# RMSNorm and matrix product on one core: the first eight tiles of the output stored as one transfer

## The chip, the cores and the metric

The kernel runs on one core of a Trainium2 chip. The metric is the device time of one launch in microseconds (us). The core has five engines with a queue of instructions each: TensorE (PE) multiplies matrices and turns tiles round, VectorE (DVE), ScalarE (ACT) and GpSimd (POOL) work on elements, and SyncE (SP) only issues transfers. Transfers between memory and the core's SBUF are carried out by 16 DMA engines that all queues share. SP and ACT each have a ring of their own on every one of the 16. A transfer is cut into packets, here one contiguous run of a partition each, and its 128 partitions are spread evenly, 8 packets to an engine.

## The reference

```python
batch, seq, dim, out_dim = 16, 1024, 512, 768
rms = np.sqrt(np.mean(x ** 2, axis=-1, keepdims=True) + eps)
x_norm = x / rms * gamma
return np.matmul(x_norm, weight).astype(np.float32)
```

There are 16384 tokens of 512 features. Each token is divided by its root mean square, scaled by gamma and multiplied by a 512 x 768 matrix. All inputs and the output are 32-bit floats: 33.6 MB of x and 1.6 MB of weight come in, 50.3 MB go out.

## The kernel before

The tokens are cut into 128 tiles of 128. Which token lands in which tile is free as long as the load and the store agree, and the helper rows() (lines 140 to 142) settles it for both: a block of t tiles is read as "(p t) d", so that a partition holds t consecutive tokens and tile number k of the block is the k-th token of every partition. The larger t, the longer the contiguous run of a partition.

Gamma goes into the weight, which is cast to bf16 once. A tile then passes through these steps:

- load (line 177): tiles 0 to 7 in transfers of 2, 2 and 4 tiles, all later ones in transfers of 8. Tiles 0 to 31 are issued at the start on SP's queue. The twelve later loads are issued on ACT's queue, each about 28 tiles ahead of use, when the buffer xt that it fills (two halves of 16 tiles) is done with.
- cast to bf16 on GpSimd (line 188), eight or four tiles at a time. The last four tiles of each sixteen are cast by line 260 into xq instead.
- sums of squares on ScalarE (line 196), then root (line 201) and reciprocal (line 203).
- the turn of the tile: by TensorE through PSUM (line 230) and a copy by VectorE (line 239), or, for the four tiles in xq, by VectorE alone in 16 moves of 32 x 32 blocks (line 271), three moves to a pair of tiles.
- eight matmuls on TensorE (line 300) into one of three PSUM accumulators.
- the scale by the reciprocal root from PSUM into the output buffer ot, on ScalarE for even tiles and on VectorE for odd ones (lines 279 and 281).
- store (line 293) by SP.

The output buffer ot has three parts of eight tiles, so tile i writes where tile i - 24 stood and waits for the store of that tile. The main loop goes over pairs of tiles (j is the pair). The kernel's class Order writes down every operation with what it reads and writes, and puts waits on semaphores where one engine, or a transfer, needs another's result; each engine works in the order in which the operations were added. No planner changes that order.

Two tables say how transfers are grouped: x_first and x_size for loads, o_first and o_size for stores. A store is issued with the last tile of its stretch:

```python
if i == first + n - 1:
    src = ot[s][:, first % OG:first % OG + n, :]
    order.transfer(SP, lambda: SP.dma_start(out=rows(out, first, n), in_=src), reads=cells("ot", s, first % OG, n))
```

The stores before are of 1, 1, 2 and 4 tiles, then thirteen of 8, and at the end three of 4 and two of 2. In the loads of tiles 0 to 7 and the stores of the same tiles, each transfer's tokens are a block of their own (t is 2, 2 and 4). Tiles 8 to 15 have eight consecutive tokens to a partition, tiles 16 to 31 sixteen, all later ones 32.

Of the kernel before, what the change touches and what calls it, by code (L numbers as in the profile page):

```python
# [100 lines left out]
def kernel(  # L101
# [22 lines left out]
    XG, OG = 16, 8  # L124
    FIRST, START, LEAD = 2 * XG, 4, 14

    def stretches(group, parts):
        first, size, i = {}, {}, 0
        for g in range(NT // group):
            for n in parts.get(g, [group]):  # L130
                for t in range(i, i + n):
                    first[t], size[t] = i, n
                i += n
        return first, size

    last = NT // OG - 1
    x_first, x_size = stretches(OG, {0: [2, 2, 4]})
    o_first, o_size = stretches(OG, {0: [1, 1, 2, 4], last - 1: [4, 4], last: [4, 2, 2]})

    def rows(ap, i, n):  # L140
        base, t = (i - i % OG, OG) if OG <= i < XG else (x_first[i], x_size[i]) if i < OG else (i - i % XG, XG) if i < 2 * XG else (i - i % (2 * XG), 2 * XG)
        return ap[base * P:(base + t) * P, :].rearrange("(p t) d -> p t d", t=t)[:, i - base:i - base + n, :]

    def sb(name, shape, dtype):
# [29 lines left out]
    def load(i):  # L174
        dst, to = x_of(i, x_size[i])
        queue = SP if i < FIRST else ACT
        order.transfer(queue, lambda: queue.dma_start(out=dst, in_=rows(x, i, x_size[i])), writes=to)  # L177
# [110 lines left out]
    def store(i):  # L288
        first, n = o_first[i], o_size[i]
        s = first // OG % 3  # L290
# [3 lines that stand above are left out]
# [188 lines left out]
```

## Time and profile before

| | |
|---|---|
| median of 3 runs | 208.84 us (208.83 to 209.33) |
| the profiled execution | 209.07 us, span 207.1 us |
| granted TensorE clock | 0.993 |
| busy: PE, DVE, ACT, POOL | 194.7, 149.5, 144.3, 60.0 us |
| moved by DMA | 85.62 MB, 413 GB/s over the span |
| stores | 22 transfers, 5.8 to 25.6 us from issue to landing, median 22.1 |
| loads of x | 18 transfers, 3.4 to 23.8 us, median 18.1 |
| last store issued, landed | 200.4, 206.2 us |

Times in rows are microseconds from the span's start. A row of a window gives busy time and number of instructions of each engine, then the granted clock, the mean busy share of the 16 DMA engines and the GB/s that they moved; the share can come out slightly over 1, because a packet counts to the stretch in which it starts and neighbouring packets overlap a little. A row of the timeline gives start, duration, engine, line, operation, output and input, and in square brackets how long the engine was idle before it and what ended that. The trace also has a record of every DMA packet: its queue, size, start and duration.

### The profile page before, as it was taken

To read this page: it belongs to the slowest core of one execution; us is meant where nothing else is said; L and a number is where in the kernel's file an instruction comes from. 1 tells how busy PE (TensorE), PEld (TensorE's weight loads), DVE (VectorE), ACT (ScalarE), POOL (GpSimd) and SP (SyncE) were. 2 spreads that over 40 slices of the span, in tenths; PEclk is the share of its full clock that TensorE was granted. 3 is DMA by queue.
4 is the path that set the end of the run, shared out by engine and by line. 5 is a ranking of instruction groups with operands and counts; after the bars stand their busy time and mean duration, and the time that the engine had idled before them with its cause. 6 is when DMAs were issued, how large, how long until landed. Compare 5 with 4: busy or idle time off the path is not lost.

```text
span 207.1 us, 2794 instructions
## 1 busy us (share of the span) xinstructions
PE 194.7 (94%) x1236; PEld 72.7 (35%) x717; DVE 149.5 (72%) x255; ACT 144.3 (70%) x343; POOL 60.0 (29%) x34
## 2 busy tenths in 40 slices
PE   7789999999999999999999999999999989999940
PEld 1233434343334334433344333443343324333310
DVE  0446556999579975999579975999569964999530
ACT  4598898777777687777777687676949758683310
POOL 2156752157006340065105170060604224000000
PEclk9999999999999999999999999999999999999997
DMA  6999999999999999999999999999999999999992
GB/s 222 402 434 453 370 419 420 426 461 407 437 429 423 449 419 440 419 434 429 432 449 411 430 434 423 445 423 437 413 424 445 427 440 435 423 437 394 394 412 120
DMA packets 6064, 85.62 MB, mean 413 GB/s; under 512 B 674, under 2 KB 676, under 8 KB 1828
## 3 DMA queue, kind: packets, MB, share of 16 engines
q1 hardware_dynamic: 4320, 60.30, 68.9%
q10 hardware_dynamic: 1732, 25.17, 28.5%
q8 instruction: 7, 0.11, 0.2%
q14 instruction: 5, 0.04, 0.0%
HBM read 35.13 MB, written 50.33 MB: 413 GB/s over the span
## 4 chain that ended last, share of the span: by engine, by line
PE 71%; DMA 17%; DVE 5%; SPq 1%; issue 1%; POOL 1%; ACT 0%; ACTq 0%
PE ps L300 63%; DMA out_dram<-ot 12%; PE ps L230 8%; DMA xt<-in_x_dram 5%; DVE ot L281 2%; DVE xTq L271 2%; DVE xT L239 1%; POOL xb L188 1%; SPq L345 0%; ACT ot L279 0%; SPq L177 0%; DVE rstd L203 0%; SPq L477 0%; ACTq L93 0%; SPq L436 0%
## 5 line engine op out<-in xcount | busy, mean ns | idle before, releaser
L300 PE MATMUL ps<-w_bf,xT 128*128 128x512 bf16 (+1 forms) x800 | 147.9, 326 | 2.1 <-DVE w_bf L281 1.1
L279 ACT ACTIVATE ot<-ps,rstd 128x768 f32<-128x768 f32 x64 | 57.6, 899 | 48.5 <-PE ps L300 37.3
L196 ACT ACTIVATE jk<-xt 128x512 bf16<-128x512 f32 x128 | 78.7, 619 | 1.9 <-DMA xt<-in_x_dram 1.9
L188 POOL CAST xb<-xt 128x2048 bf16<-128x2048 f32 (+3 forms) x21 | 46.4, 2218 | 112.4 <-PE ps L230 69.0
L281 DVE TENSOR_SCALAR ot<-ps,rstd 128x768 f32<-128x768 f32 x64 | 64.8, 1013 | 9.5 <-PE ps L300 8.1
L296 PEld LDWEIGHTS <-xT 128*128 128x128 bf16 x400 | 39.3, 98 | 60.7 <-issue 52.8
L230 PE MATMUL ps<-ident_f,xb 128*128 128x128 f32 x200 | 54.4, 276 | 0.9 <-POOL xb L188 0.9
L239 DVE COPY xT<-ps 128x1024 bf16<-128x1024 bf16 (+1 forms) x53 | 34.5, 654 | 24.2 <-PE ps L230 22.5
L271 DVE STREAM_TRANSPOSE xTq<-xq 32x256 f32<-32x256 f32 x112 | 48.8, 435 | 3.4
L230 PEld LDWEIGHTS ps<-ident_f,xb 128*128 128x128 f32 x200 | 28.3, 143 | 46.6 <-issue 43.3
L300 PE MATMUL ps<-w_bf,xTq 128*128 128x512 bf16 x224 | 42.8, 326 | 0.0
L196 ACT ACTIVATION_READ_ACCUMULATOR jk<-xt 128x1 f32 x128 | 24.4, 190 | 0.0
L296 PEld LDWEIGHTS <-xTq 128*128 128x128 bf16 x112 | 11.0, 98 | 14.5 <-issue 14.5
L260 POOL CAST xq<-xt 128x2048 bf16<-128x2048 f32 x7 | 13.3, 1893 | 0.0
L203 DVE RECIPROCAL rstd<-rms 128x8 f32<-128x8 f32 (+3 forms) x20 | 3.9, 193 | 8.1 <-ACT rms L201 7.9
L201 ACT ACTIVATE rms<-ssq,eps_sb 128x8 f32<-128x8 f32 (+3 forms) x20 | 6.0, 300 | 0.6
L300 PE MATMUL ps<-warm 128*128 128x512 bf16 x10 | 4.5, 588 | 1.4 <-DVE eps_sb L354 1.4
L279 ACT ACTIVATE w_bf<-w_f,g_sb 128x768 bf16<-128x768 f32 x2 | 1.9, 935 | 1.8 <-DMA w_f<-in_weight_dram 1.8
L377 DVE COPY g_sb<-ps 128x4 f32<-128x4 f32 x1 | 0.2, 163 | 3.2 <-PE ps L371 3.2
L341 ACT ACT_TABLE_LOAD x1 | 1.3, 1283 | 1.5 <-SPq L436 1.5
L281 DVE TENSOR_SCALAR w_bf<-w_f,g_sb 128x512 bf16<-128x512 f32 (+2 forms) x3 | 1.4, 482 | 1.2 <-DMA w_f<-in_weight_dram 1.2
L371 PEld LDWEIGHTS ps<-ident_f,g_row 2*128 2x128 f32 x2 | 0.3, 200 | 2.6 <-issue 2.6
(10 smaller groups left out, 2.0 us busy)
## 6 DMA issues: line engine op xcount, KB each, us to landing
out_dram<-ot SPq DMA_DIRECT2D x13, 3072.0 KB, 22.7
xt<-in_x_dram ACTq DMA_DIRECT2D x12, 2048.0 KB, 18.8
xt<-in_x_dram SPq DMA_DIRECT2D x3, 2048.0 KB, 18.2
out_dram<-ot SPq DMA_DIRECT2D x4, 1536.0 KB, 10.9
out_dram<-ot SPq DMA_DIRECT2D x3, 768.0 KB, 6.8
w_f<-in_weight_dram SPq DMA_DIRECT2D x2, 768.0 KB, 5.9
xt<-in_x_dram SPq DMA_DIRECT2D x2, 512.0 KB, 5.4
xt<-in_x_dram SPq DMA_DIRECT2D x1, 1024.0 KB, 9.5
```

What stands on the lines that cost most here:

```text
L188: run(POOL, lambda: POOL.tensor_copy(out=xb[s][:, i % 8:i % 8 + n, :], in_=src), of, cells("xb", s, i % 8, n))
L196: run(ACT, lambda: ACT.activation(out=jk[j], in_=src[:, 0, :], func=AF.Square, accum_out=ssq[:, i:i + 1]), of, [("jk", j), ("ssq", i)])
L201: run(ACT, lambda: ACT.activation(out=rms[:, s], in_=ssq[:, s], func=AF.Sqrt, scale=1.0 / D, bias=eps_sb), [("ssq", t) for t in range(i, i ...
L203: run(DVE, lambda: DVE.reciprocal(out=rstd[:, s], in_=rms[:, s]), [("rms", i)], [("rstd", t) for t in range(i, i + n)])
L230: run(PE, lambda: PE.transpose(out=tp[b][:, t, h, :], in_=words[:, lo:lo + P], identity=ident_f), cells("xb", s, j % 4 * 2 + t) + ["ident" ...
L239: run(DVE, lambda: DVE.tensor_copy(out=dst[:, t:t + n, :], in_=src[:, t:t + n, :]), [("tp", b)], cells("xT", j % 4, t, n))
L260: run(POOL, lambda: POOL.tensor_copy(out=xq[s], in_=src), of, [("xq", s)])
L271: run(DVE, lambda: DVE.transpose(out=dst, in_=src), [("xq", s)], [("xTq", s)])
L279: run(ACT, lambda: ACT.mul(out=dst, in_=src, mul=r), reads, writes)
L281: run(DVE, lambda: DVE.tensor_single_scalar(out=dst, in_=src, scalar=r, op=mybir.AluOpType.mult), reads, writes)
L296: run(PE, lambda: PE.ldweights(lhsT), [cell])
L300: run(PE, lambda: PE.add_instruction(mybir.InstMatmult(name=nc.get_next_instruction_name(), engine=mybir.EngineType.PE, ins=[PE.lower_ap(r ...
```

## The change

The first group of stores, tiles 0 to 7, is no longer cut in four: it is one transfer of 3 MB, issued after tile 7. For that the eight tiles must be one block, so rows() gives them eight consecutive tokens to a partition, as tiles 8 to 15 have. The loads use the same helper. They stay three transfers of 2, 2 and 4 tiles with the same packet sizes (4, 4 and 8 KB), but each now fetches its part of a row of eight tokens, pieces that stand 16 KB apart in memory, where each used to fetch one solid stretch.

```diff
-    o_first, o_size = stretches(OG, {0: [1, 1, 2, 4], last - 1: [4, 4], last: [4, 2, 2]})
+    o_first, o_size = stretches(OG, {last - 1: [4, 4], last: [4, 2, 2]})
 
     def rows(ap, i, n):
-        base, t = (i - i % OG, OG) if OG <= i < XG else (x_first[i], x_size[i]) if i < OG else (i - i % XG, XG) if i < 2 * XG else (i - i % (2 * XG), 2 * XG)
+        t = OG if i < XG else XG if i < 2 * XG else 2 * XG
+        base = i - i % t
         return ap[base * P:(base + t) * P, :].rearrange("(p t) d -> p t d", t=t)[:, i - base:i - base + n, :]
```

The packets of a store are 3 KB times its tiles: those of the four early stores were 3, 3, 6 and 12 KB, that of the one transfer is 24 KB, as in every other store of eight tiles. The order of the instructions on PE, DVE, ACT and POOL stays; on SP four issues become one.

## The prediction

> **What bounds the kernel now.** I read the busy slices first, then the windows by stage, the waits of ScalarE, the queues, and last the trace's records of single DMA packets.
>
> ```profile
> PEclk9999999999999999999999999999999999999997
> DMA  6999999999999999999999999999999999999992
> DMA packets 6064, 85.62 MB, mean 413 GB/s; under 512 B 674, under 2 KB 676, under 8 KB 1828
> q1 hardware_dynamic: 4320, 60.30, 68.9%
> q10 hardware_dynamic: 1732, 25.17, 28.5%
> ```
>
> The 16 DMA engines are busy from the first slices to the last but one, and the two queues (q1 is SP's, q10 is ScalarE's) fill 97.4% of the span between them. The clock is full, so it is no suspect.
>
> ```profile
> core 0: us, PE busy (x) PEld busy (x) DVE busy (x) ACT busy (x) POOL busy (x), PEclk, DMA share, GB/s
> 20.00:30.00 10.00, 10.00 (x69) 4.19 (x41) 5.75 (x10) 9.31 (x26) 6.33 (x3) 1.00 1.00 398
> 150.00:160.00 10.00, 9.98 (x67) 3.96 (x39) 7.98 (x14) 6.49 (x17) 2.03 (x1) 1.00 1.01 433
> 160.00:170.00 10.00, 9.23 (x60) 3.10 (x32) 8.62 (x16) 6.18 (x16) 1.97 (x2) 1.00 1.01 432
> 190.00:200.00 10.00, 9.05 (x56) 2.64 (x27) 6.08 (x9) 3.59 (x4) 0.00 (x0) 1.00 0.94 393
> ```
>
> TensorE and the DMA engines are both full. TensorE loses 0.8 us in the middle (9.98 and 9.23 of 10), and ScalarE's rows (start, duration, idle time before and who ended it) say why:
>
> ```profile
> 143.19 0.90 ACT L279 ACTIVATE ot<-ps,rstd 128x768 f32<-128x768 f32 x1 [1.85 <-DMA out_dram<-ot]
> 155.59 0.90 ACT L279 ACTIVATE ot<-ps,rstd 128x768 f32<-128x768 f32 x1 [2.98 <-DMA out_dram<-ot]
> 168.01 0.90 ACT L279 ACTIVATE ot<-ps,rstd 128x768 f32<-128x768 f32 x1 [3.07 <-DMA out_dram<-ot]
> ```
>
> A group of eight tiles waits for the store that frees its output buffer, every 12.4 us: DMA can't keep pace with TensorE's 11.7 us per group.
>
> Which one ends last is told by the packet records. The last store is issued at 200.40 and lands 5.8 us later, at 206.2. Fifteen engines finish their last packet between 203.3 and 203.5; one runs without a gap from 201.98 to 205.74, sixteen 6 KB packets end to end. That engine is slower on the stores: its 24 KB packets take 0.944 us (median), those of the others 0.912. So the end is the work of one slow DMA engine, which is behind by 2.3 us and has nothing to wait for.
>
> **The change, part by part.** The sum is made against the profiled execution: span 207.1, time 209.07, which is 0.23 above the median of 208.84.
>
> *Stores removed and added.* Every transfer puts 8 packets on each engine. Packet medians are 121 ns (3 KB), 234 (6 KB), 460 (12 KB) and 912 (24 KB). Before: 16 x 0.121 + 8 x 0.234 + 8 x 0.460 = 7.49 us of an engine. After: 8 x 0.912 = 7.30. That is 0.19 less, and three semaphore records of 9 ns fewer are 0.03: 0.22 us on an ordinary engine. On the slow one the 12 KB packets of the early store take 0.474 on average and the small ones are not slower: 1.94 + 1.88 + 3.79 = 7.61 against 8 x 0.944 = 7.55, with the records 0.08 to 0.09 us. The end is the slow engine's, so the gain is between 0.08 and 0.22; I take 0.14, since the slow engine's handful of early packets is a thin sample.
>
> *SP's issues.* Four issues (12.48, 13.53, 17.05, 24.41; 0.33 us each) become one, after tile 7, at the same 24.41. SP has nothing else to do then; the next issue is at 36.23. Nothing.
>
> *When the bytes move.* The early stores do not move early now. They stand on SP's ring behind the loads of tiles 0 to 31, whose packets end at 26.84; the first 3 KB packet starts at 26.63. So issuing at 24.41 instead of 12.48 leaves no hole, provided that the new store is ready by 26.6: at the end of the run an idle engine took up the store issued at 200.40 at about 201.5, 1.1 us after, which gives 25.5. Cover: 1.1 us; if the loads end 0.5 us sooner, 0.6.
>
> *Who shares with whom.* The two rings take turns packet by packet: from 43.8 on the slow engine's records alternate 0.912-like and 0.611 (the 16 KB of a load), and eight rounds are 12.13 us, the distance of successive stores. Between 27 and 42 the stores' packets are small, so the loads run ahead: the first three on q10 run 27.46 to 33.11, 34.54 to 41.59 and, after 4 us with no load, 45.58 to 56.99. With 24 KB packets on the other ring each takes some 11.4 us and starts 12.13 after the one before: 27.5 to 38.9, to 51.0, to 63.1. Loads from the third on come 6.1 us later. The stores gain what they lose: that of tiles 8 to 15 ended at 55.65 and now ends near 26.7 + 2 x 12.13 = 51.0, 4.7 us sooner. No byte is added.
>
> *The stall that goes.* Stores 4.7 us sooner take away waits of 1.6 to 3.1 us on ot, and with them TensorE's 0.8 us. What is late next is the loads.
>
> *The wait that comes.* GpSimd takes a load as soon as it lands, and DVE takes what GpSimd cast:
>
> ```profile
> 169.60 1.89 POOL L188 CAST xb<-xt 128x2048 bf16<-128x2048 f32 x1 [8.03 <-DMA xt<-in_x_dram]
> 171.44 1.89 POOL L260 CAST xq<-xt 128x2048 bf16<-128x2048 f32 x1
> 177.74 1.36 DVE L271 STREAM_TRANSPOSE xTq<-xq 32x256 f32<-32x256 f32 x3
> ```
>
> The last load, tiles 120 to 127, is issued at 147.36 and lands at 169.5; 6.1 later is 175.6. Two casts take it to 179.4, where DVE wanted the last quad at 177.7, or 176.9 with the 0.8 us gone: DVE waits 1.7 to 2.5 us. Behind that wait in its queue stand the copy xT<-ps (TensorE's transposes wait for it) and the odd tiles' scale. DVE is full from there to 193, so I count all of it: last store issued between 200.4 - 0.8 + 0 and 200.4 - 0.8 + 2.5, that is 199.6 to 202.1. An undisturbed last store needs 1.1 us to start, 8 x 0.234 = 1.9 to move and up to 0.5 to land, so 203.1 to 205.6, under the slow engine's 206.2 - 0.14. Cost: nothing, hidden by the slow engine's backlog. The margin is 0.5 us at the bad end.
>
> *Reads of tiles 0 to 7.* The helper rows() also serves the loads: the three transfers (2, 2, 4 tiles) now fetch 4 KB or 8 KB pieces that stand 16 KB apart, where each was one solid stretch. Packet sizes stay. Bounds: the first load's 4 KB packets average 0.207 us, the second's 0.161. If all of the second and third paid that 0.046 per 4 KB, it is 8 x 0.046 + 8 x 0.092 = 1.1 us more; if the first stopped paying, 0.4 less. I take nothing: tiles 16 on are read in 16 KB pieces 32 or 64 KB apart at the 0.611 of a solid stretch.
>
> Sum: 209.07 - 0.14 = 208.93 on the profiled run's footing, 208.70 on the median's.
>
> A transfer on an idle engine spends 1.1 us before its first packet and 0.5 us after its last. In a ring that is never empty the records show neither: the next transfer's packets follow within 0.01 us. So I count no fixed cost per transfer. The Trainium skill speaks for more: "DMA: Bandwidth & Descriptors" gives a transfer about 2.0 us of fixed cost in its section "Anatomy of one DMA — SWDGE (gpsimd) path" (measured on GpSimd's path; SP issues these), and its "Rules for kernel authors" advise coalescing many small transfers into one. By that, three transfers fewer would be an estimated 6 us, and the sum 202.7 instead of 208.7.
>
> **The rivals.**
>
> *Late loads become the bound (slower).* For it: DVE has 0.4 us idle at most between 177.7 and 193, and the margin is 0.5 us. Against: TensorE can run some tiles ahead, and the margin counts every stall in full. It decides from a landing of the last load past about 176.2. With 8 us in place of 6.1: landing 177.5, casts done 181.3, DVE waits 3.6 to 4.4, last store issued at 204.0, end at 207.5 in place of 206.2: 210.1.
>
> *Scattered reads cost (slower).* Half the bound on top and more: 209.4 to 209.8.
>
> *The slow reads at 24 go (faster).*
>
> ```profile
> 22.00:24.00 2.00, 2.00 (x16) 0.86 (x10) 1.24 (x2) 1.59 (x6) 1.62 (x1) 1.00 0.95 401
> 24.00:26.00 2.00, 2.00 (x15) 0.86 (x9) 0.99 (x3) 1.72 (x4) 1.98 (x1) 1.00 1.00 311
> ```
>
> In that window all engines are busy and move 311 instead of 432 GB/s: 2 x (1 - 311/432) = 0.56 us lost, on 16 KB load packets. If the 3 KB stores waiting behind them cause it, the change gives 0.56 back on every engine: 208.1. Against: nothing shows the link.
>
> *Fixed cost per transfer (faster).* If the ring stood still for those 1.1 + 0.5 us at each transfer, three fewer would save 4.8: 203.9. Against: no such gap in the records. The rule of the skill named above is of this kind.
>
> **How the numbers follow.** About 0.3% (0.63 us) is what a measurement of this kernel can tell from no change: 208.21 to 209.47. Chances: forecast 0.52, late loads 0.24, scattered reads 0.06, slow reads gone 0.15, fixed cost 0.03. So faster 0.18, within 0.52, slower 0.30. The likeliest case alone spans 208.3 to 209.0. The range runs from 207.9 (slow reads gone, with the full 0.22 of the packets and the first load's 0.4 in part) to 210.1 (late loads as priced), and leaves out the worse half of the late loads and the fixed cost, 0.15.
>
> **What will show it.** Right: one 3072 KB store issued near 24.4 and no idle DMA slice at 26; store landings near 17 to 20 us in mid-run instead of 22 to 25, load landings near 24 to 28 instead of 18 to 22; no ScalarE wait on out_dram<-ot before 160; GpSimd's waits on xt longer; one engine still last. Wrong: a last store issued after 202 (late loads), 4 and 8 KB packets over 0.2 and 0.35 us (scattered reads), or more than 400 GB/s in 24 to 26 (slow reads gone).

## The result: slower by 0.8%, and the profile after

| | before | changed |
|---|---|---|
| median of all runs | 209.06 us (17 runs, 208.57 to 210.65) | 211.97 us (17 runs, 209.84 to 220.18) |
| ratio, changed to before | | 1.0077, 95% interval 1.0055 to 1.0099 |
| the profiled execution, span | 209.07 us, 207.1 us | 212.54 us, 210.5 us |
| stores of 3 MB, issue to landing, median | 22.7 us | 21.1 us |
| loads on ACT's queue, issue to landing, median | 18.8 us | 24.4 us |

The changed kernel is slower, by 1.2 to 2.1 us, and the predicted range (up to 210.1) does not hold its time. Executions in a slower state of the chip, 7 of the changed kernel's 17, are in the median but not in the ratios here and below, and by the ratio the time is about 210.7 us. The profiled execution is the slowest of the other ten, so a second profile of the same kernel, at 210.34 us (span 208.3), is read beside it.

The first view is the list of windows: busy time and instructions of each engine, the clock, the mean share of the DMA engines and what they moved. First the changed kernel:

```profile
core 0: us, PE busy (x) PEld busy (x) DVE busy (x) ACT busy (x) POOL busy (x), PEclk, DMA share, GB/s
0.00:24.00 24.00, 21.06 (x104) 6.84 (x64) 9.27 (x23) 16.79 (x40) 9.47 (x14) 1.00 0.92 374
24.00:26.00 2.00, 2.00 (x15) 0.82 (x9) 1.30 (x3) 1.30 (x5) 2.00 (x1) 1.00 0.98 418
26.00:28.00 2.00, 2.00 (x16) 0.80 (x9) 1.61 (x2) 2.00 (x8) 0.82 (x1) 1.00 1.10 303
28.00:30.00 2.00, 2.00 (x16) 0.82 (x8) 0.66 (x2) 2.00 (x6) 0.89 (x1) 1.00 0.84 274
100.00:170.00 70.00, 68.70 (x444) 25.95 (x258) 55.07 (x93) 49.69 (x121) 22.01 (x9) 1.00 1.01 423
180.00:190.00 10.00, 9.09 (x60) 3.56 (x35) 7.15 (x13) 6.68 (x17) 2.45 (x2) 1.00 0.94 403
190.00:200.00 10.00, 9.42 (x58) 2.86 (x29) 8.57 (x15) 3.24 (x4) 0.00 (x0) 1.00 0.84 353
```

and the same stretches of the kernel before that have not been shown yet:

```profile
0.00:24.00 24.00, 20.44 (x110) 7.13 (x68) 10.11 (x24) 17.20 (x41) 10.29 (x14) 1.00 0.93 381
26.00:28.00 2.00, 2.00 (x15) 0.73 (x8) 1.09 (x2) 2.00 (x7) 0.00 (x0) 1.00 0.97 392
28.00:30.00 2.00, 2.00 (x15) 0.82 (x8) 1.49 (x2) 2.00 (x6) 1.58 (x1) 1.00 1.04 442
100.00:170.00 70.00, 69.21 (x450) 26.12 (x260) 56.42 (x96) 50.10 (x121) 18.66 (x8) 1.00 1.01 431
180.00:190.00 10.00, 10.00 (x67) 3.85 (x38) 9.54 (x17) 5.53 (x15) 0.00 (x0) 1.00 0.99 425
```

Read the last column. Between 100 and 170 us the DMA engines are full in both (share 1.01), and move 423 GB/s in the changed kernel, 431 in the one before. In the first 30 us the slow stretch of the kernel before, 311 GB/s at 24 to 26, is gone (418), and 26 to 30 has become slow in its place: 303 and 274 GB/s (295 and 336 in the repeat). Full engines that move less: their packets take longer.

The second view is the timeline at the end (start, duration, engine, line, operation; idle time before it and who ended that). It answers to the rows of GpSimd and VectorE shown in the prediction:

```profile
148.11 0.33 ACTq L178 DMA_DIRECT2D xt<-in_x_dram  x1
178.71 1.90 POOL L189 CAST xb<-xt 128x2048 bf16<-128x2048 f32 x1 [9.28 <-DMA xt<-in_x_dram]
180.55 1.90 POOL L261 CAST xq<-xt 128x2048 bf16<-128x2048 f32 x1
182.48 1.37 DVE L272 STREAM_TRANSPOSE xTq<-xq 32x256 f32<-32x256 f32 x3 [2.58 <-POOL xq L261]
```

The last load lands at 178.6 in place of 169.5, 30.5 us after its issue. VectorE, which had waited for nothing there, now stands 2.6 us, and TensorE loses 0.9 us of the window 180 to 190 (9.09 for 10.00). The last store is issued at 204.68 (200.40 before). The repeat shows the same at 176.46 (GpSimd's cast), 2.63 us and 202.43.

The third is the list of waits (total us, times, longest):

```profile
POOL xb L189 <- DMA xt<-in_x_dram: 112.7, 17, 9.5
ACT ot L280 <- DMA out_dram<-ot: 7.0, 4, 2.4
DVE xTq L272 <- POOL xq L261: 5.3, 2, 2.7
```

and in the kernel before, where the third of these does not occur:

```profile
POOL xb L188 <- DMA xt<-in_x_dram: 37.9, 10, 8.0
ACT ot L279 <- DMA out_dram<-ot: 9.5, 4, 3.1
```

GpSimd's waits on loads have grown from 37.9 us to 112.7, as the taking of turns says. The waits of ScalarE on the output buffer have shrunk, but they have not gone. The three longest, in the timeline:

```profile
143.94 0.90 ACT L280 ACTIVATE ot<-ps,rstd 128x768 f32<-128x768 f32 x1 [1.77 <-DMA out_dram<-ot]
156.66 0.90 ACT L280 ACTIVATE ot<-ps,rstd 128x768 f32<-128x768 f32 x1 [2.28 <-DMA out_dram<-ot]
169.56 0.90 ACT L280 ACTIVATE ot<-ps,rstd 128x768 f32<-128x768 f32 x1 [2.43 <-DMA out_dram<-ot]
```

The queues, from the page, fill 96.8% of a longer span (97.4% before) with fewer packets (5632 for 6064) and the same bytes:

```profile
DMA packets 5632, 85.62 MB, mean 407 GB/s; under 512 B 626, under 2 KB 628, under 8 KB 1396
q1 hardware_dynamic: 3888, 60.29, 68.2%
q10 hardware_dynamic: 1732, 25.17, 28.6%
```

The packet records do not name the engine; it has to be followed from one packet's end to the next one's start. At the end fourteen engines finish at 207.4 to 207.7 and two at 209.0 and 209.3 (before: fifteen at 203.3 to 203.5 and one at 205.7). The run of packets that ends last follows a gap and starts only at 199.9. So with a share of 0.84 in the window 190 to 200 the engines have work to wait for: the last tiles are late, not only one engine.

### The profile page after: what moved, and what is told of

Its sections match the earlier page's. It is cut to its first block, busy times and chain, and to the rows that moved or that the text cites. A ratio compares the mean times of both kernels' runs of the same rounds, so it can differ in the third digit from the quotient of the medians.

```text
span 210.5 us, 2786 instructions
## 1 busy us (share of the span) xinstructions
PE 197.4 (94%) x1236; PEld 72.7 (35%) x717; DVE 149.5 (71%) x255; ACT 145.0 (69%) x343; POOL 60.0 (29%) x34
## 2 busy tenths in 40 slices
DMA packets 5632, 85.62 MB, mean 407 GB/s; under 512 B 626, under 2 KB 628, under 8 KB 1396
## 4 chain that ended last, share of the span: by engine, by line
PE 59%; DMA 19%; DVE 12%; ACT 3%; POOL 2%; issue 2%; SPq 1%; POOLq 0%
PE ps L301 52%; DMA xt<-in_x_dram 19%; PE ps L231 7%; DVE ot L282 5%; DVE xTq L272 5%; DVE xT L240 2%; ACT jk L197 2%; POOL xb L189 1%; POOL xq L261 1%; ACT ot L280 1%; SPq L178 0%; SPq L346 0%; DVE rstd L204 0%; ACT rms L202 0%; SPq L478 0%
## 5 line engine op out<-in xcount | busy, mean ns | idle before, releaser
L301 PE MATMUL ps<-w_bf,xT 128*128 128x512 bf16 (+1 forms) x800 | 149.7, 327 | 2.9 <-DVE ot L282 2.4
L189 POOL CAST xb<-xt 128x2048 bf16<-128x2048 f32 (+3 forms) x21 | 46.5, 2221 | 121.4 <-DMA xt<-in_x_dram 112.7
## 6 DMA issues: line engine op xcount, KB each, us to landing
out_dram<-ot SPq DMA_DIRECT2D x14, 3072.0 KB, 21.1
xt<-in_x_dram ACTq DMA_DIRECT2D x12, 2048.0 KB, 24.4
```

The costliest lines, as they stand in the source:

```text
L189: run(POOL, lambda: POOL.tensor_copy(out=xb[s][:, i % 8:i % 8 + n, :], in_=src), of, cells("xb", s, i % 8, n))
L301: run(PE, lambda: PE.add_instruction(mybir.InstMatmult(name=nc.get_next_instruction_name(), engine=mybir.EngineType.PE, ins=[PE.lower_ap(r ...
```

## The experiments

Ratios are to runs of the kernel before on the same chip, with 95% intervals.

**The change repeated.**

> The changed kernel once more, beside the others on one chip. If its long runs (up to 220 us) belong to the kernel, they come again, with a median above 210 us; if they were chance, it is near 210.2 us with a spread of 1 us. In the profile, last landing of a load past 176 us goes with a last store issued after 202 us; a run whose loads land sooner ends near 210.

210.47 us, 1.0070 (1.0044 to 1.0096). The result stands, and this profile is the one that the others are compared with.

**The layout alone**: rows() as changed, the four early stores as before, whose pieces now stand 24 KB apart in memory too.

```diff
     o_first, o_size = stretches(OG, {0: [1, 1, 2, 4], last - 1: [4, 4], last: [4, 2, 2]})
     def rows(ap, i, n):
-        base, t = (i - i % OG, OG) if OG <= i < XG else (x_first[i], x_size[i]) if i < OG else (i - i % XG, XG) if i < 2 * XG else (i - i % (2 * XG), 2 * XG)
+        t = OG if i < XG else XG if i < 2 * XG else 2 * XG
+        base = i - i % t
```

> The new token layout of tiles 0 to 7 in loads and stores, but the four early stores kept. If the scattered reads and pieces cost by themselves (first load's 4 KB packets at 0.27 us and more, first landing 1.3 us later, some 0.5 us of DMA time lost before 5 us), this kernel is 0.5 to 1 us slower than the kernel before and has that first landing. If the late single store is the whole cause, it equals the kernel before within 0.2 us; its stores start near 26.6 us and its loads run ahead as before (last load's landing about 22 us after issue).

209.67 us, 1.0044 (1.0018 to 1.0070). Last load at 171.9, last store issued at 201.34.

**Four late stores**: the old layout, the four old stores, meant to be issued after tile 7.

```diff
     def store(i):
+        if i < OG - 1:
+            return
+        for last_of in [0, 1, 3, 7] if i == OG - 1 else [i]:
+            store_one(last_of)
+
+    def store_one(i):
```

> The old layout and the four old stores with their small packets, but all four issued after tile 7 (near 24.4 us) instead of at 12.5, 13.5, 17.1 and 24.4. If issuing late is what costs (the ring of stores then starts some 4 us after issue, near 29 us, and DMA moves only some 300 GB/s from 24 to 30 us), this kernel is 0.5 to 1 us slower than before. If the 24 KB packets are what costs, by pushing the loads back, its loads still run ahead (last load about 22 us to landing) and its time equals that of the kernel before within 0.2 us.

209.18 us, 1.0009 (0.9982 to 1.0035). But the edit did not make the stores late. It changes only the place at which they are written down, and SP has nothing else to issue there, so each still goes out when its own tile is done. The row of SP's issues, first of this run and then of the kernel before (five transfers within 24.08 us of the first issue):

```profile
11.78 24.08 SPq L299 DMA_DIRECT2D out_dram<-ot  x5
12.48 24.08 SPq L293 DMA_DIRECT2D out_dram<-ot  x5
```

They are issued at 11.78, 12.83, 16.35 and 23.71, where the kernel before has 12.48, 13.53, 17.05 and 24.41, and all engines have the instructions of the kernel before in the same order. So this is that kernel run again, and it says nothing on late issue. It is of use below, as a measure of how far two executions of the same work lie apart.

**The reads alone, and the store alone.** In the first of these only the loads of tiles 0 to 7 use the eight-token layout, in the second only the store does (as one transfer). Load and store then disagree, so the first 1024 tokens of the output stand in another order; the work is the same. The edit of the reads is shown; for the store it is the store's rows() that gets True, and o_first is that of the change.

```diff
-    def rows(ap, i, n):
+    def rows(ap, i, n, wide=False):
+        if wide and i < OG:
+            return ap[:OG * P, :].rearrange("(p t) d -> p t d", t=OG)[:, i:i + n, :]
...
-        order.transfer(queue, lambda: queue.dma_start(out=dst, in_=rows(x, i, x_size[i])), writes=to)
+        order.transfer(queue, lambda: queue.dma_start(out=dst, in_=rows(x, i, x_size[i], True)), writes=to)
```

> Only the loads of tiles 0 to 7 use the new layout; the stores are those of before, so the first 1024 tokens come out in another order (that part of the result is not the reference's). If scattered reads cost, 0.5 to 1 us slower than before with the first load landing about 1.3 us later; if that late landing in the changed kernel was chance, equal within 0.2 us.

> Only the store uses the new layout: one transfer after tile 7, while the loads of tiles 0 to 7 read solid stretches as before, so the first 1024 tokens come out in another order (that part of the result is not the reference's). If the single late store is the whole cause, this kernel is as slow as the changed one (1.3 to 1.6 us above before, with the same tail of longer runs); if the reads are the cause, it equals the kernel before; if both share, about 0.6 us.

Reads alone: 209.30 us, 1.0023 (1.0010 to 1.0036). Store alone: 209.51 us, 1.0028 (1.0017 to 1.0038), with the last load at 175.9, VectorE waiting 1.90 us and the last store issued at 201.99. Each costs about a third of the loss; that the two together come to 0.5% and the change to 0.7 or 0.8% is not clear of the intervals. Part of the price of the reads sits in the first load. The timeline gives ScalarE's first square in the run with the reads alone and then in that with the store alone, whose reads are solid:

```profile
5.63 0.63 ACT L198 ACTIVATE jk<-xt 128x512 bf16<-128x512 f32 x1 [2.85 <-DMA xt<-in_x_dram]
```

```profile
4.39 0.63 ACT L198 ACTIVATE jk<-xt 128x512 bf16<-128x512 f32 x1 [1.61 <-DMA xt<-in_x_dram]
```

The first load lands 1.24 us later when its pieces are scattered.

**Other ways to cut the store, in the new layout**: one tile and then seven (21 KB packets); four and four (12 KB); eight of one tile (3 KB), meant to be issued after tile 7. The edit of the first is shown; the others differ in the list for group 0 (`[4, 4]` and `[1] * 8`), and the last has the store() of the four late stores as well.

```diff
-    o_first, o_size = stretches(OG, {last - 1: [4, 4], last: [4, 2, 2]})
+    o_first, o_size = stretches(OG, {0: [1, 7], last - 1: [4, 4], last: [4, 2, 2]})
```

> The changed kernel with tile 0 stored early as before and tiles 1 to 7 as one late transfer (21 KB packets). If the slow stretch from 26 to 29 us comes from the store's ring being empty when ScalarE's load starts, or from the first touch of the output's memory, the early store takes it away: over 390 GB/s in 24 to 30 us and 0.4 to 0.6 us less than the changed kernel. If it comes from the big late store itself (starting some 4 us after issue), it stays near 340 GB/s and the time is that of the changed kernel. Loads are as late as in the changed kernel either way.

> The changed kernel with two stores of four tiles (12 KB packets), the first issued after tile 3 near 17 us, so that it stands ready when the loads of tiles 0 to 31 end. Theory late loads: the loads gain some 2 us on the changed kernel (12 KB against 16 KB packets), the long tail goes, 209.5 to 209.8 us, the rest over the kernel before being the scattered first read. Theory that only the first read counts: the same. Theory that the late issue counts and not the packets: under 209.7 as well, but with loads as late as in the changed kernel.

> The changed kernel with the one store cut in eight transfers of one tile (3 KB packets), all issued after tile 7. The packets cost an engine 64 x 0.121 = 7.74 us instead of 8 x 0.912 = 7.30, so 0.4 us more of DMA work. If the changed kernel is slow because the store's big packets push the loads back, this one has loads that land about 22 us after issue, no long tail, and 209.8 to 210.1 us, less than the changed kernel in spite of the work. If the issue time or the reads do it, it is 0.4 us slower than the changed kernel.

One and seven: 210.17 us, 1.0066 (1.0038 to 1.0095). Four and four: 209.05 us, 0.9999 (0.9981 to 1.0017). Eight small: 209.36 us, 1.0019 (0.9997 to 1.0041), although its packets are 64 x 0.121 = 7.74 us of an engine in place of 7.30. So the number of transfers does not cost the time. Large first packets go with the loss and small ones do not, but packet size is not parted from time of issue here: the eight small ones went out one by one as their tiles were done, from 13.31 to 25.24, the two of four at 17.74 and 25.12, and the one store of the change at 25.24. No run has small packets that all wait for tile 7. Windows of one and seven, then of four and four:

```profile
24.00:30.00 6.00, 5.95 (x41) 2.44 (x24) 3.57 (x6) 5.48 (x16) 4.10 (x2) 1.00 1.00 407
100.00:170.00 70.00, 69.53 (x447) 26.55 (x263) 56.96 (x96) 51.70 (x126) 22.01 (x9) 1.00 1.00 421
```

```profile
24.00:30.00 6.00, 6.00 (x41) 2.37 (x25) 3.57 (x7) 5.31 (x14) 3.97 (x2) 1.00 0.98 376
100.00:170.00 70.00, 69.53 (x447) 26.47 (x263) 57.03 (x96) 51.48 (x125) 18.28 (x7) 1.00 1.01 430
```

One and seven has no slow stretch at 24 to 30 and is as slow as the change all the same, because it loses more later (421 GB/s). Its first 3 KB packets stood ready on SP's ring when the loads there ended (first one at 26.3), and the 21 KB packets followed at 29.0 without a pause. So the slow stretch at 26 to 30 does not come with large packets as such; it comes where SP's ring runs empty first. Four and four loses in neither place.

**The kernel before with later loads.** Nothing is changed but that each load on ACT's queue after the first is issued two pairs later.

```diff
-    FIRST, START, LEAD = 2 * XG, 4, 14
+    FIRST, START, LEAD = 2 * XG, 4, 12
```

> The kernel before, layout and stores untouched, with the loads from tile 40 on issued two pairs (5.9 us) later: LEAD 12 instead of 14. It makes loads late and changes nothing else. Theory late loads: the last load lands near 175 to 177 us instead of 169.5, DVE waits on GpSimd's xq cast, the last store is issued after 201.5 us, and the time is 0.3 to 0.8% above before, as in the changed kernel. Theory that late loads are hidden and something else in the single store costs: equal to the kernel before within 0.2%, with landings as late.

The profiled execution took 211.22 us: last load at 176.4, VectorE waiting 1.58 us, last store issued at 202.47, much like the change. But the seven runs in the ratio reach from 208.74 to 211.22 and give 1.0004 (0.9980 to 1.0029), so the profile shows the slowest of them. At this point I still held late loads for the cause, since that profile shows their marks; the ratio did not bear it out.

**The loads given back their place.** These two decide it. Both are the changed kernel, with one later store cut into two of four tiles: that of tiles 8 to 15, or that of tiles 72 to 79. Smaller store packets let the loads run ahead.

```diff
-    o_first, o_size = stretches(OG, {last - 1: [4, 4], last: [4, 2, 2]})
+    o_first, o_size = stretches(OG, {1: [4, 4], last - 1: [4, 4], last: [4, 2, 2]})
```

(and `9: [4, 4]` in place of `1: [4, 4]`)

> The changed kernel with one edit: the store of tiles 8 to 15 is cut into two of four tiles. Its packets are 12 KB, so for eight rounds of turns the load ring gets more than before; the single store of tiles 0 to 7 and the new layout stay. More packet work: 8 x (2 x 0.460 - 0.912) = 0.06 us. Theory (late loads push the end): loads of 16 KB gain up to 8 x 0.45 = 3.6 us of place, so the last load lands at 173 to 175 instead of 176.4 to 178.7, VectorE's wait for the last xq falls from 2.6 us below 1.5, and the time falls to 209.3 to 210.0 (ratio 1.001 to 1.005). Rival (the single store or the scattered reads cost the time at the front, whatever the loads do later): the last load may come earlier, the time stays at 210.4 to 210.7 (ratio 1.006 to 1.008).

> The changed kernel with one edit: the store of tiles 72 to 79, in the middle of the run, is cut into two of four tiles. The front is the changed kernel's to the last packet until some 130 us. Theory (late loads push the end): the loads after it gain up to 3.6 us, the last one lands at 173 to 175, VectorE's wait for the last xq falls below 1.5 us, and the time falls to 209.3 to 210.0 (ratio 1.001 to 1.005), as in the run with the second group halved. Rival (the front costs the time): 210.4 to 210.7 (ratio 1.006 to 1.008), with the last load earlier all the same.

1.0056 (1.0036 to 1.0077) and 1.0078 (1.0042 to 1.0114); the profiled executions took 210.15 and 211.47 us. Timeline and waits of the first of the two:

```profile
169.91 1.89 POOL L189 CAST xb<-xt 128x2048 bf16<-128x2048 f32 x1 [4.01 <-DMA xt<-in_x_dram]
```

```profile
POOL xb L189 <- DMA xt<-in_x_dram: 33.3, 10, 5.2
ACT ot L280 <- DMA out_dram<-ot: 21.4, 8, 3.5
```

The last load lands at 169.8, earlier than I expected (173 to 175) and as early as before the change; VectorE no longer waits for xq there. Yet the last store is issued at 203.80, and the time is that of the change. What the loads gained the stores lost: ScalarE now waits for them eight times, 21.4 us. That alone does not make a kernel slow: the four late stores have 20.4 us of such waits and the two, two and four below 19.3, at the time of the kernel before. In the chain of work that ended last (start, us, what) the longest piece of the repeated change is the last load, and with the second group halved it is a store:

```profile
147.53 28.80 DMA xt<-in_x_dram
```

```profile
96.34 25.78 DMA out_dram<-ot
...
132.04 27.80 DMA out_dram<-ot
```

With the tenth group halved it is one wait of 5.55 us at 171. The clock was granted in full in the changed kernel, but in this run it shows 0.83 at 170 to 180, behind that wait:

```profile
170.00:180.00 10.00, 7.86 (x40) 2.81 (x24) 4.30 (x6) 6.74 (x17) 3.08 (x2) 0.83 1.01 432
```

So the theory of late loads falls as the sole cause; the rival set against it put the loss at the front alone, and the next part shows that to be half to two thirds of it.

**What all of them have in common.** From the packet records (size, start, duration) I added up what the DMA engines of each kernel had moved by a given time, and compared it with the kernel before. The difference is told in us, at the 430 KB per us that it moves in mid-run; each row comes from one profiled execution, and those of the change, the reads alone and the later loads are their kernel's slowest in the ratio. The four late stores are the kernel before once more, so their row shows what chance does to a column: up to 0.6.

| kernel | lost before 24 | 24 to 30 | 30 to 170 | behind at 170 | ratio |
|---|---|---|---|---|---|
| two, two, four (below) | -0.20 | 0.18 | 0.07 | 0.04 | 0.9982 |
| four late stores | -0.43 | -0.28 | 0.63 | -0.07 | 1.0009 |
| four and four | 0.47 | -0.03 | -0.06 | 0.38 | 0.9999 |
| layout alone | 0.60 | -0.54 | 0.40 | 0.45 | 1.0044 |
| later loads | -0.22 | -0.15 | 0.98 | 0.62 | 1.0004 |
| eight small | 0.54 | -0.36 | 0.50 | 0.67 | 1.0019 |
| reads alone | 0.52 | -0.48 | 0.91 | 0.96 | 1.0023 |
| store alone | -0.26 | 0.50 | 0.73 | 0.97 | 1.0028 |
| second group halved | 0.40 | 0.43 | 0.39 | 1.22 | 1.0056 |
| change, repeated | 0.48 | 0.50 | 0.47 | 1.45 | 1.0070 |
| one and seven | 0.52 | -0.42 | 1.77 | 1.87 | 1.0066 |
| tenth group halved | 0.44 | 0.23 | 1.43 | 2.11 | 1.0078 |
| change | 0.55 | 0.53 | 1.25 | 2.34 | 1.0077 |

The five slowest kernels are the five that are furthest behind, and the correlation of the last two columns is 0.89. Since every kernel moves the same 85.62 MB through engines that are full from 24 to 170 us, whoever is behind there ends late; that the shares of the two rings decide whether a load or a store shows it is my reading. The layout alone (1.0044, 0.45 us behind) and the later loads (1.0004, 0.62) do not fit well. Nor is this all of the loss in every execution: the first profile of the change is 2.3 us behind at 170 and 4.0 at 200, and that of the later loads 0.6 and 2.0. Both end behind a late last load, with a DMA share of 0.84 and 0.83 at 190 to 200. There, as far as these two profiles show, the late load does cost on top.

The loss has three places. The scattered first load costs 0.4 to 0.6 us in every kernel that has it, against the kernel before; the other kernels with solid reads are 0.2 to 0.4 ahead of that one, so it may be up to 1.0. The one store of 24 KB packets, which finds SP's ring empty, costs 0.2 to 0.5 net at 24 to 30 in the five kernels that have it. And from 30 to 170, 24 KB store packets that take over 1.05 us in place of 0.912 become more: 4 in the kernel before and in four and four, 36 and 68 in the two profiles of the change, 93 with one and seven. The 68 take 0.30 us too long on average: 68 x 0.30 / 16 = 1.3 us of each engine, the whole of the change's third column. They do not need the one large store: the reads alone, whose stores are those of before, have 60. And most stand where the engines pass from one store to the next: in the change 45 of the 68 are among the last 32 of a transfer's 128 packets in order of start, and 12 among the first 16.

**Two, two and four**: the kernel before, with its two stores of one tile joined.

```diff
-    o_first, o_size = stretches(OG, {0: [1, 1, 2, 4], last - 1: [4, 4], last: [4, 2, 2]})
+    o_first, o_size = stretches(OG, {0: [2, 2, 4], last - 1: [4, 4], last: [4, 2, 2]})
```

> The kernel before with its two stores of one tile made one of two tiles (6 KB packets). Theory late loads: packets of 6 KB leave the loads nearly as far ahead as 3 KB ones, so within 0.15% of before, perhaps 0.05 us less for the packets saved. If every merging of stores costs, slower by 0.1% or more.

208.86 us, 0.9982 (0.9966 to 0.9998): 0.18% below the kernel before, less than the 0.3% that the prediction took as the least that can be told.

## Why the prediction was wrong

- **Packets, 0.14 us less.** Not isolated. The plain 24 KB packets kept their 0.912 us, but the term took every packet at its median; the 36 to 68 packets over 1.05 us outweigh it many times.
- **SP's issues, "leaves no hole".** This step failed. It let the store start 1.1 us after its issue, as it does on idle engines. Its first packet came 4.5 us after it (25.24 to 29.76). The loads in front of it had left SP's ring by 26.8 on half of the engines, and until 29.76 the other ring ran with some thirty packets that took about twice 0.611. That is the 303 and 274 GB/s shown above: 1.0 us lost at 26 to 30, with 0.5 won back at 24 to 26. The issue was 0.8 us later than forecast, but that is not the reason: with the store alone it came at 24.00, before the forecast, and the first packet at 28.40. The kernel before had a better price on record: its first load on ACT's queue, issued at 23.33 beside SP's full ring, has its first packet at 27.4, 4.1 us after.
- **Reads of tiles 0 to 7, "I take nothing".** Wrong by 0.5 us, inside its own bound (1.1) but at another place: not the second and third load, the first pays more. With the solid reads of the store alone the loss before 24 us is gone.
- **Turns packet by packet.** Right. On the fast engines the first three loads on ACT's ring end at 37.0, 49.1 and 61.3 (38.9, 51.0 and 63.1 forecast) in place of 33.1, 40.9 and 56.8, and GpSimd's waits tripled.
- **The stall on ot goes.** Partly: 9.5 us of waits became 3.4 in the repeat and 7.0 in the first profile. The stores gained less than forecast: that of tiles 8 to 15 ended 1.6 to 2.1 us sooner, not 4.7.
- **The wait that comes, "nothing, hidden by the slow engine's backlog".** The sequence was right and even the sizes were near: VectorE waits 2.6 us (forecast 1.7 to 2.5), the last store goes out at 202.43 in the repeat (at most 202.1). But 175.6 for the last load took the 3 us by which the slowest engine trails the fastest as fixed; it was 5.4 and 7.4 us, and the load landed at 176.3 and 178.6. Nor is the end the slow engine's alone any more: its last run of packets began after a gap, at 199.9, and with the second group halved all sixteen engines finish within 0.3 us, behind the last tiles.
- **The rivals.** Late loads: sign, marks and price (210.1) came out, but loads that were on time again did not bring the time back, so as a cause it was not enough. Slow reads at 24: its sign, over 400 GB/s at 24 to 26, came true (418), and still the time was not gained, since the slow stretch moved to 26 to 30. With the layout alone it went without return, and gave back 0.54 us of the 0.60 lost before. Scattered reads: real, 0.23% alone, not by the packets I named: only the first load's grew, from 0.207 us to 0.249, and the sign of over 0.2 was met before the change already. Fixed cost per transfer: against the sign; cutting the store in two gave 0.9999, the one transfer 1.0070.

Under all this lies one assumption: "no byte is added", so the engines' work was taken as unchanged but for packet medians, and only its order was followed. The order was right, and the rate was not: the engines lost 1.5 to 2.3 us by 170, and nothing hides that in a kernel that they bound.

## What to carry to other kernels

Where DMA engines are full from end to end, sum up the bytes moved over time first: a wait that appears or goes elsewhere only shows which queue carries the deficit, and curing it moves the wait to the other queue. A change in packet size is a change of the shares between rings. The rate of the engines is no constant either: in the profile of the reads alone, where no packet size was changed, it fell in mid-run (0.91 us lost). Price a transfer's start by a start beside a running ring, and try sizes in between (four and four, or two, two and four) before the largest. And look in the trace whether an edit did what it was meant to do: a store that is written down later is not issued later if its queue only waits for its data.

## What was not expected of the hardware

- A transfer on SP's empty ring needed 3.6 to 4.5 us from issue to first packet while ACT's ring was running (five runs), against 1.1 us on idle engines. The Trainium skill, "DMA: Bandwidth & Descriptors", section "Specifications", gives some 0.6 us to the first byte for this path; all of these measured numbers are above it.
- While a ring starts, packets of the other can take twice their time: 16 KB loads 1.0 to 1.3 us on average instead of 0.611, one or two per engine. It is seen just before the start of either ring (24 to 26 us before the change, 26 to 30 after). Why the packets slow down is open.
- The first load is slow when its 4 KB pieces lie 16 KB apart (236 to 255 GB/s at 2 to 5 us, 352 to 380 with solid reads), the second is not. Whether it is that the load's pieces are spread over 2 MB instead of 512 KB, no run separates.
- One DMA engine trails, and how far depends on the schedule: on the last load by 2.9 to 3.6 us in the kernel before, four late stores, four and four, eight small, two, two and four and the second group halved; by 5.4 to 7.4 in the change, one and seven, the later loads and the tenth group halved; by 4.1 to 4.9 in the others.
- Why 24 KB store packets become slow, in the change above all from 100 us on, is open. Issuing the loads later, with no other edit, raised their number from 4 to 44, and scattering the first reads to 60, so the timing of the loads has a part in it.
